# A tuned two-layer hybrid mixer on Trainium2: row-tiled shift products, a 512-wide running maximum and transposed broadcast columns in the attention loop

## The chip, the cores and the metric

One core of one Trainium2 chip runs the whole program. The metric is the device time in microseconds (us). The kernel before took 1449.69 us (median of 3 runs, 1438.94 to 1453.29).

## The reference, cut to what matters

Two layers work on 1024 latent tokens and 256 context tokens of width 1024. Each layer normalises its tokens, multiplies by one combined input projection and sends the slices to four mixers: latent attention, pooling, a state space and a spatial gate. Their outputs are gated and go through one output projection. The change touches the attention alone. Its inputs pass an RMS norm, and it is a softmax attention with 4 heads over 1280 keys for the latent queries (in the first layer also over 256 keys for the context queries):

```python
def _rms(x, g):
    return x * lax.rsqrt(jnp.mean(x * x, -1, keepdims=True) + LN_EPS) * g

s = einsum('bqhd,bkhd->bhqk', qn, k_nope) + einsum('bqhr,bkr->bhqk', qr, k_rope)
p = softmax(s * scale, axis=-1)
o = einsum('bhqk,bkhd->bqhd', p, vf)
```

## The kernel before, in words

Each layer runs in three stages: the input projection with the other mixers' work filled in between (`layer`), the attention loop (`attention`), and the output projection (`out_proj`). Products of float32 values are made of three float32r products (`mm3`: high by high, high by low, low by high).

**The norm (`rms`, L1074).** The squares are summed over features by products with a column of ones (L1084), `r` holds the factor of 128 tokens in each of up to four columns, and L1095 spreads it: a matmul with the column, broadcast to 128 columns, as stationary operand and the identity as moving operand gives a tile in which every row holds the 128 factors. There are 11 such calls (3 for the keys and 3 for the queries in layer 0, 3 and 2 in layer 1) with 38 column spreads in all. They stand in the input-projection stage, where the order of the instructions is a planner's.

**The attention loop (`attention`, L1476 to L1526).** Its order is written out by hand for PE, DVE, ACT and POOL (`manual_schedule`): each engine works in the order of the program. Work is cut into units of 256 queries by one pair of heads (`pairs`). Layer 0 has 8 latent units and 2 context units, layer 1 has 8 latent units. An iteration `w` does one head of a unit, so there are 20 and 16 iterations, of which 32 are full (latent) and 4 short (context). What an iteration does, in the order of the code:

- `scores(v, h, range(1, 5))` (L1314): four banks of scores of the present head, each 128 keys by 2 by 256 queries in one 512-wide PSUM bank, 6 products a bank (L1330). Bank 0 of this head was scored in the iteration before. The running maximum `acc` starts as ACT's copy of bank 0 (`first`, L1338), then DVE takes the maximum with each half of each bank (L1335 to L1340, 8 operations of 256 columns), and folds the two halves (L1342).
- The finish of the unit before and the query projections of the next unit (`finish`, `q_chunk`, `q_pair`) are generators which `go(...)` advances at marked places.
- `vals`: the product of probabilities and values for the head before (`values`, L1400, L1411). It has 5 key-tile pairs, that is 10 products an iteration, two instructions each. `PVS` says how they are cut into three places: 2, 3 and 0 key tiles (3, 2 and 0 in every fourth iteration).
- `maxima` (L1349), after the first place: two PE transposes turn `acc` (L1354), DVE reduces to a maximum for each query (`mx`, L1356), and two small operations make the negated maximum in a high and a low part (`m`, L1358, L1359).
- `rows` (L1361), after the second place: one PE transpose of the four columns (L1365), then one DVE operation makes the rows (`row`, L1367).
- `scores(..., range(0, 1))` for the next head's bank 0 (L1501), then the third place and the `finish` steps: `tp_sm` (L1431, sums over keys) and DVE's reciprocal (L1435).
- `shift` (L1369): five products with a contraction of 4 rows, one on each bank, add the negated maximum to the scores (L1376). Then ACT takes the five exponentials (L1389) into `pE`, `pL`, `pM`, with `first` for the next head after the second of them, and POOL adds them up (`psum`).

The loop draws its PSUM from 5 banks of tag `mm` and 2 of tag `tp`; every sixth score bank is a `tp` bank.

Of the kernel before, what the change touches and what calls it, by code (L numbers as in the profile page):

```python
# [12 lines left out]
F32 = mybir.dt.float32  # L13
F32R = mybir.dt.float32r
I32 = mybir.dt.int32
AF = mybir.ActivationFunctionType
ALU = mybir.AluOpType
AX = mybir.AxisListType
# [15 lines left out]
NPOS = 161  # L34
SEG = 32
PFIX = (1, 2, 3)
PVS = (((0, 2), (2, 5), (5, 5)), ((0, 2), (2, 5), (5, 5)), ((0, 2), (2, 5), (5, 5)), ((0, 3), (3, 5), (5, 5)))
VW = ((0, 1, None), (2, 3, None))
CX = 2
POW = ((0, 4), (4,))  # L40
# [35 lines left out]
def tile_hybrid_backbone(ctx: ExitStack, tc: tile.TileContext, A):  # L76
    nc = tc.nc
    V, S, P, T, D = nc.vector, nc.scalar, nc.gpsimd, nc.tensor, nc.sync

    const = ctx.enter_context(tc.tile_pool(name="const", bufs=1))  # L80
    big = ctx.enter_context(tc.tile_pool(name="big", bufs=1))
    wk = ctx.enter_context(tc.tile_pool(name="wk", bufs=2))
    sml = ctx.enter_context(tc.tile_pool(name="sml", bufs=4))
# [16 lines left out]
    stg = [""]  # L100
# [29 lines left out]
    def tt(e, out, a, b, op):  # L130
        return e.tensor_tensor(out=out, in0=a, in1=b, op=op)  # L131

    def mul(e, out, a, b):
        return tt(e, out, a, b, ALU.mult)

    def add(e, out, a, b):
        return tt(e, out, a, b, ALU.add)
# [4 lines left out]
    def ts(e, out, a, s1, op0, s2_=None, op1=None):  # L142
        if op1 is None:
            return e.tensor_scalar(out=out, in0=a, scalar1=s1, scalar2=None, op0=op0)  # L144
        return e.tensor_scalar(out=out, in0=a, scalar1=s1, scalar2=s2_, op0=op0, op1=op1)  # L145

    def stt(out, a, s, b, op0, op1):
        return V.scalar_tensor_tensor(out=out, in0=a, scalar=s, in1=b, op0=op0, op1=op1)  # L148
# [8 lines left out]
    ident = const.tile([128, 128], F32, name="ident")  # L157
# [4 lines left out]
    V.memset(ones, 1.0)  # L162
    edge = const.tile([128, 2, 18], F32, name="edge")
    D.dma_start(edge, A["edge"])
    rmask = const.tile([4, 2], F32, name="rmask")
    add(V, rmask, ident[0:4, 0:2], ident[0:4, 2:4])
    ones4 = const.tile([4, 128], F32R, name="ones4")
    V.tensor_copy(ones4, ones[0:4, :].to_broadcast([4, 128]))


    cv = s2("cv")[0:16, 0:128]
# [902 lines left out]
    def rms(raws, nfeat, gains):  # L1074

        def go(t0, n):
            nt = n // 128
            stg[0] = "rms"
            ps = tp_ps()
            for j, (x, k) in enumerate(raws):  # L1080
                sq = s2("sq")
                S.activation(out=sq[0:k, 0:n], in_=x[0:k, t0:t0 + n], func=AF.Square)
                for i in range(nt):
                    T.matmul(ps[:, 8 * i + j:8 * i + j + 1], lhsT=sq[0:k, 128 * i:128 * i + 128], rhs=ones[0:k, 0:1],  # L1084
                             start=True, stop=True)
            r = sml.tile([128, 4], F32, tag="rrs", name="rrs")
            pv = ps[:, 0:8 * nt].rearrange("p (i j) -> p i j", j=8)
            ts(V, r[:, 0:nt], pv[:, :, 0], 1.0 / nfeat, ALU.mult, EPS, ALU.add)
            if len(raws) == 2:
                stt(r[:, 0:nt], pv[:, :, 1], 1.0 / nfeat, r[:, 0:nt], ALU.mult, ALU.add)  # L1090
            with tc.high_priority():
                tt(P, r[:, 0:nt], r[:, 0:nt], mhalf.to_broadcast([128, nt]), ALU.pow)
            ps = tp_ps()
            for i in range(nt):
                T.matmul(ps[:, 128 * i:128 * i + 128], lhsT=r[:, i:i + 1].to_broadcast([128, 128]), rhs=ident,  # L1095
                         start=True, stop=True)
            r = ps
            for (x, k), g in zip(raws, gains):
                stt(x[0:k, t0:t0 + n], x[0:k, t0:t0 + n], g, r[0:k, 0:n], ALU.mult, ALU.mult)
        return go  # L1100
# [113 lines left out]
    def attention(l, last, blocks, out):  # L1214
# [99 lines left out]
        def scores(v, h, banks):  # L1314

            c0, pr = pairs[v]
            stg[0] = "sc"
            K, Q = KT[2 * pr + h][(slice(0, 96), slice(0, 128))[h]], prep[v][h]
            if 0 in banks:
                st[v, h] = dict(b=[], acc=s2("acc"))  # L1320
            d = st[v, h]
            acc = d["acc"]
            for i, kts in list(enumerate(BANKS if c0 < NLAT else BANKS[0:1]))[banks.start:banks.stop]:
                ps = tp_ps() if nb[0] % 6 == 5 else mm_ps()
                nb[0] += 1
                d["b"].append(ps)
                for x, kt_ in enumerate(kts):
                    out = ps[:, n * x:n * x + n]
                    for y, (e, f) in enumerate(((0, 0), (0, 1), (1, 0))):
                        T.matmul(out, lhsT=K[:, e, 128 * kt_:128 * kt_ + 128], rhs=Q[:, f], start=(x == 0 and y == 0),  # L1330
                                 stop=False, skip_group_check=True)
                if c0 == NLAT:
                    V.tensor_reduce(out=acc[:, 0:n], in_=ps.rearrange("p (x q) -> p q x", x=2), axis=AX.X, op=ALU.max)
                    continue
                for x in range(2):  # L1335
                    a, p = acc[:, n * x:n * x + n], ps[:, n * x:n * x + n]
                    if i == 0:
                        d["first"] = lambda: S.copy(acc, d["b"][0])  # L1338
                    else:
                        tt(V, a, a, p, ALU.max)  # L1340
                if i == 4:
                    tt(V, acc[:, 0:n], acc[:, 0:n], acc[:, n:2 * n], ALU.max)  # L1342

# [5 lines left out]
        def maxima(v, h):  # L1349
            d = st[v, h]  # L1350
            stg[0] = "mx"
            d["tp"] = tp = tp_ps()
            for j in range(2):
                T.transpose(tp[:, 128 * j:128 * j + 128], d["acc"][:, 128 * j:128 * j + 128], ident)  # L1354
            m = sml.tile([128, 2], F32, tag="mx", name="mx")
            V.tensor_reduce(out=m, in_=tp[:, 0:n].rearrange("p (j k) -> p j k", j=2), axis=AX.X, op=ALU.max)  # L1356
            d["m4"] = m4 = sml.tile([128, 4], F32, tag="m4", name="m4")
            ts(V, m4[:, 0:2].bitcast(F32R), m, -1.0, ALU.mult)  # L1358
            stt(m4[:, 2:4], m, -1.0, m4[:, 0:2], ALU.mult, ALU.subtract)  # L1359

        def rows(v, h):  # L1361

            d = st[v, h]
            tp = d["tp"][0:4, 256:384]
            T.transpose(tp, d["m4"], ident)  # L1365
            d["row"] = row = sml.tile([4, 2, 128], F32R, tag="row", name="row", bufs=2)
            mul(V, row, tp.unsqueeze(1).to_broadcast([4, 2, 128]), rmask.unsqueeze(2).to_broadcast([4, 2, 128]))  # L1367

        def shift(v, h):  # L1369

            c0, pr = pairs[v]
            d = st[v, h]
            stg[0] = "sh"
            rv = d["row"].rearrange("p j q -> p (j q)").unsqueeze(1).to_broadcast([4, 2, n])
            for ps in d["b"]:
                T.matmul(ps, lhsT=ones4, rhs=rv, start=False, stop=True, skip_group_check=True)  # L1376
            e, l1, l2 = wh("pE", F32), None, None
            pt = d["pt"] = [e[:, 0:512], e[:, 512:1024]]
            if c0 < NLAT:
                l1 = wr("pL")  # L1380
                if v < nv - 1:
                    l2 = qp[0].tile([128, 512], F32, tag="pM", name="pM", bufs=3)
                else:
                    if h == 0:
                        st["pM"] = wr("pM")
                    l2 = st["pM"][:, 512 * h:512 * h + 512]
                pt += [l1[:, 0:512], l1[:, 512:1024], l2]
            for i, (ps, p) in enumerate(zip(d["b"], pt)):
                S.activation(out=p, in_=ps, func=AF.Exp, scale=QSCALE)  # L1389
                if i == (1 if c0 < NLAT else 0):  # L1390
                    first(v + h, 1 - h)
            sm = d["sm"] = qp[0].tile([128, 512], F32, tag="psum", name="psum", bufs=3) if v < nv - 1 else s2("psum")
            if c0 < NLAT:
                for i in range(1, 5):
                    add(P, sm, pt[0] if i == 1 else sm, pt[i])
                add(P, sm[:, 0:n], sm[:, 0:n], sm[:, n:2 * n])
            else:
                add(P, sm[:, 0:n], pt[0][:, 0:n], pt[0][:, n:2 * n])
# [77 lines left out]
        with tc.manual_schedule(engines={mybir.EngineType[x] for x in MAN}):  # L1476
            for w in range(2 * nv):
# [13 lines left out]
                    start(q_pair(v + 1, *pairs[v + 1]))  # L1491
                go("mm")
                go("act mm")
                k = [range(5 * h + i, 5 * h + j) for i, j in PVS[w % 4]]
                vals(v, w, k, 0)
                maxima(v, h)
                go("m4")
                vals(v, w, k, 1)
                rows(v, h)
                go("row")  # L1500
                if w + 1 < 2 * nv:  # L1501
                    scores((w + 1) // 2, 1 - h, range(0, 1))
                vals(v, w, k, 2)
                if h and short:
                    go("fend")
# [9 lines left out]
                if w == 2 * nv - 1:  # L1515
                    drop("attq", "att")
                    out.alloc()
                    out.split()
                shift(v, h)
                if w == 2 * fresh[-1] - 3:  # L1520
                    out.scales()
                if w == 2 * nv - 4:
# [528 lines left out]
```

## Time and profile before

| what | value |
|---|---|
| time, median of 3 runs | 1449.69 us (1438.94 to 1453.29) |
| the profiled execution's own time | 1443.26 us |
| its span, first to last instruction | 1441.5 us |
| mean granted TensorE clock, of full speed | 0.940 |
| attention loop of layer 0, in the span | 481 to 672 us |
| attention loop of layer 1, in the span | 1177 to 1339 us |

The span is 1.8 us less than the profiled execution's time. PE is the matmul engine and PEld its weight loads, which overlap with it. In the chain of waits each line is a piece of the path that ended last, with its start, its length and who was at work.

### The profile page before, as it was taken

To read this page: it belongs to the slowest core of one execution; us is meant where nothing else is said; L and a number is where in the kernel's file an instruction comes from. 1 tells how busy PE (TensorE), PEld (TensorE's weight loads), DVE (VectorE), ACT (ScalarE), POOL (GpSimd) and SP (SyncE) were. 2 spreads that over 40 slices of the span, in tenths; PEclk is the share of its full clock that TensorE was granted. 3 is DMA by queue.
4 is the path that set the end of the run, shared out by engine and by line. 5 is a ranking of instruction groups with operands and counts; after the bars stand their busy time and mean duration, and the time that the engine had idled before them with its cause. 6 is when DMAs were issued, how large, how long until landed. Compare 5 with 4: busy or idle time off the path is not lost.

```text
span 1441.5 us, 20269 instructions
## 1 busy us (share of the span) xinstructions
PE 1271.1 (88%) x7558; PEld 992.0 (69%) x7558; DVE 937.8 (65%) x1974; ACT 464.8 (32%) x879; POOL 552.8 (38%) x580
## 2 busy tenths in 40 slices
PE   4877986999999998999999769987699999999997
PEld 1555764779888766766777657765488787766785
DVE  8685399623552576757799882699426447767566
ACT  2341220120343644445233422301213454544300
POOL 2476241301002345655444591314001126656343
PEclk9988997999998999999999979998799999999999
DMA  9435321665321100014122454412752020000421
GB/s 314 143 103 179 122 86 46 152 178 132 89 53 33 27 22 1 1 45 131 45 82 95 107 155 147 122 44 59 149 146 65 8 59 23 15 16 16 146 103 73
DMA packets 124679, 127.33 MB, mean 88 GB/s; under 512 B 40908, under 2 KB 98724, under 8 KB 124582
## 3 DMA queue, kind: packets, MB, share of 16 engines
q1 hardware_dynamic: 118886, 111.86, 26.3%
q0 software_dynamic: 2880, 9.54, 2.8%
q10 hardware_dynamic: 2816, 4.65, 0.9%
q8 instruction: 59, 0.97, 0.3%
q14 instruction: 38, 0.31, 0.1%
HBM read 97.47 MB, written 25.94 MB: 86 GB/s over the span
## 4 chain that ended last, share of the span: by engine, by line
PE 51%; DVE 28%; issue 7%; POOL 6%; DMA 3%; ACT 3%; SPq 1%; POOLq 0%; ACTq 0%; DVEq 0%
PE mm_sc L1330 7%; PE mm_out L1632 6%; PE mm_in L154 5%; PE mm_in L152 5%; DVE H L131 5%; PE mm_in L153 5%; PE av L1411 3%; DVE stmp L131 3%; DVE z L148 3%; PE mm_sc L1376 2%; DVE op L131 2%; DVE acc L131 2%; POOL op L131 1%; DVE xres L145 1%; PE tp_sc L1330 1%
## 5 line engine op out<-in xcount | busy, mean ns | idle before, releaser
L154 PE MATMUL mm_in<-hT,wlo 128*128 128x512 f32 (+1 forms) x696 | 264.6, 381 | 26.9 <-DVE wlo L131 26.9
L152 PE MATMUL mm_in<-hT,whi 128*128 128x512 f32 (+1 forms) x696 | 270.4, 390 | 0.4 <-ACT whi L635 0.4
L153 PE MATMUL mm_in<-hT,whi 128*128 128x512 f32 (+1 forms) x696 | 264.8, 381 | 5.8 <-POOL hT L131 3.1
L154 PEld LDWEIGHTS mm_in<-hT,wlo 128*128 128x128 f32 x696 | 137.6, 198 | 53.3 <-DVE wlo L131 29.4
L152 PEld LDWEIGHTS mm_in<-hT,whi 128*128 128x128 f32 x696 | 137.8, 199 | 35.8 <-issue 14.2
L1632 PE MATMUL mm_out<-wo,yh 128*128 128x512 f32 x576 | 161.4, 394 | 0.5 <-POOL wo L131 0.4
L153 PEld LDWEIGHTS mm_in<-hT,whi 128*128 128x128 f32 x696 | 138.2, 199 | 31.1 <-POOL hT L131 5.7
L1632 PEld LDWEIGHTS mm_out<-wo,yh 128*128 128x128 f32 x576 | 107.5, 189 | 25.5 <-issue 1.0
L635 ACT CAST whi<-wraw 128x1024 fp32r<-128x1024 f32 x38 | 42.6, 1122 | 192.4 <-PE mm_in L153 142.8
L131 DVE TENSOR_TENSOR acc<-acc,mm_sc 128x256 f32<-128x256 f32 x216 | 77.4, 417 | 39.9 <-PE mm_sc L1330 36.8
L131 DVE TENSOR_TENSOR wlo<-wraw,whi 128x1024 fp32r<-128x1024 f32 x38 | 58.0, 1532 | 67.1 <-ACT whi L635 61.0
L131 POOL TENSOR_TENSOR psum<-pE 128x512 f32<-128x512 f32 (+1 forms) x36 | 47.1, 1308 | 135.8 <-ACT pE L1389 135.8
L1632 PE MATMUL mm_out<-wo,yl 128*128 128x512 f32 x288 | 92.0, 392 | 0.6 <-POOL yl L131 0.6
L131 POOL TENSOR_TENSOR psum<-psum,pL 128x512 f32<-128x512 f32 x64 | 83.1, 1298 | 5.0
L131 DVE TENSOR_TENSOR H<-H,stmp 128x80 f32<-128x80 f32 x248 | 75.2, 362 | 0.8
L131 DVE TENSOR_TENSOR stmp<-a,H 128x160 f32<-128x160 f32 x124 | 54.8, 476 | 14.5 <-POOL pws L131 7.2
L144 POOL TENSOR_SCALAR srs<-smv 128x1 f32<-128x1 f32 x18 | 5.6, 312 | 152.6 <-DVE smv L1062 152.6
L1389 ACT ACTIVATE pE<-mm_sc 128x512 f32<-128x512 f32 x55 | 30.6, 594 | 102.3 <-PE mm_sc L1376 102.3
L1632 PEld LDWEIGHTS mm_out<-wo,yl 128*128 128x128 f32 x288 | 54.3, 189 | 12.5 <-POOL yl L131 1.0
L144 POOL TENSOR_SCALAR rs_z<-mv_z 128x1 f32<-128x1 f32 x18 | 18.5, 1029 | 114.7 <-DVE mv_z L1664 114.7
L1783 ACT ACTIVATE G<-mm_in 128x512 f32<-128x512 f32 (+1 forms) x40 | 22.2, 554 | 115.9 <-PE mm_in L154 115.9
L1330 PE MATMUL mm_sc<-QA,KT 96*128 96x256 f32 x372 | 56.8, 305 | 0.0
(360 smaller groups left out, 2805.8 us busy)
## 6 DMA issues: line engine op xcount, KB each, us to landing
wmod<-in_w_mod_dram SPq DMA_DIRECT2D x48, 512.0 KB, 4.5
wraw<-in_w_in_dram SPq DMA_DIRECT2D x36, 512.0 KB, 4.4
wor<-in_w_out_dram SPq DMA_DIRECT2D x16, 512.0 KB, 3.6
s5u<-Sd SPq DMA_DIRECT2D x8, 640.0 KB, 7.1
xd<-z SPq DMA_DIRECT2D x10, 512.0 KB, 2.7
xin<-in_x_dram SPq DMA_DIRECT2D x8, 512.0 KB, 7.6
Ed<-E ACTq DMA_DIRECT2D x16, 256.0 KB, 3.2
Rd<-bldR POOLq DMA_DIRECT2D x16, 256.0 KB, 3.9
```

Source lines behind the costliest of these rows:

```text
L131: return e.tensor_tensor(out=out, in0=a, in1=b, op=op)
L144: return e.tensor_scalar(out=out, in0=a, scalar1=s1, scalar2=None, op0=op0)
L148: return V.scalar_tensor_tensor(out=out, in0=a, scalar=s, in1=b, op0=op0, op1=op1)
L152: T.matmul(out, lhsT=ahi, rhs=bhi, start=start, stop=False)
L153: T.matmul(out, lhsT=ahi, rhs=blo, start=False, stop=False)
L154: T.matmul(out, lhsT=alo, rhs=bhi, start=False, stop=stop)
L635: copy(hi, raw)
L1330: T.matmul(out, lhsT=K[:, e, 128 * kt_:128 * kt_ + 128], rhs=Q[:, f], start=(x == 0 and y == 0), stop=False, skip_group_check=True)
L1376: T.matmul(ps, lhsT=ones4, rhs=rv, start=False, stop=True, skip_group_check=True)
L1389: S.activation(out=p, in_=ps, func=AF.Exp, scale=QSCALE)
L1411: T.matmul(st[v][64 * h:64 * h + 64, 0:n], lhsT=Vt[:, BANKS[i // 2][i % 2], 64 * head:64 * head + 64], rhs=st[v, h]["pt"][i // 2][:, n * ( ...
L1632: T.matmul(a[1][nh], lhsT=y[u][:, k, :], rhs=self.W[k][:, v, 512 * nh:512 * nh + 512], start=(k == 0 and u == 0 and v == 0), stop=(k == KC ...
```

## The change

The diff, cut to its core; tables and lines that stay are left out.

```diff
-PVS = (((0, 2), (2, 5), (5, 5)), ((0, 2), (2, 5), (5, 5)), ((0, 2), (2, 5), (5, 5)), ((0, 3), (3, 5), (5, 5)))
+PVS = ((0, 2), (2, 3), (3, 5))
...
-    rmask = const.tile([4, 2], F32, name="rmask")
-    add(V, rmask, ident[0:4, 0:2], ident[0:4, 2:4])
-    ones4 = const.tile([4, 128], F32R, name="ones4")
-    V.tensor_copy(ones4, ones[0:4, :].to_broadcast([4, 128]))
+    par = const.tile([128, 2], F32, name="par")
+    V.tensor_reduce(out=par[:, 1:2], in_=ident.rearrange("p (c r) -> p r c", r=2)[:, 1:2, :], axis=AX.X, op=ALU.add)
+    ts(V, par[:, 0:1], par[:, 1:2], 2.0, ALU.mult, -1.0, ALU.add)
+    ts(V, par[:, 1:2], par[:, 1:2], -1.0, ALU.mult)
+    ones4 = const.tile([128, 128], F32R, name="ones4")
+    V.tensor_copy(ones4, ones.to_broadcast([128, 128]))
...
-                T.matmul(ps[:, 128 * i:128 * i + 128], lhsT=r[:, i:i + 1].to_broadcast([128, 128]), rhs=ident,
-                         start=True, stop=True)
+                T.transpose(ps[:, 128 * i:128 * i + 128], r[:, i:i + 1].to_broadcast([128, 128]), ident)
...
-                for x in range(2):
-                    a, p = acc[:, n * x:n * x + n], ps[:, n * x:n * x + n]
-                    if i == 0:
-                        d["first"] = lambda: S.copy(acc, d["b"][0])
-                    else:
-                        tt(V, a, a, p, ALU.max)
+                if i == 0:
+                    d["first"] = lambda: S.copy(acc, d["b"][0])
+                else:
+                    tt(V, acc, acc, ps, ALU.max)
...
-            m = sml.tile([128, 2], F32, tag="mx", name="mx")
+            d["m"] = m = sml.tile([128, 2], F32, tag="mx", name="mx")
...
-            d["m4"] = m4 = sml.tile([128, 4], F32, tag="m4", name="m4")
-            ts(V, m4[:, 0:2].bitcast(F32R), m, -1.0, ALU.mult)
-            stt(m4[:, 2:4], m, -1.0, m4[:, 0:2], ALU.mult, ALU.subtract)
...
-            tp = d["tp"][0:4, 256:384]
-            T.transpose(tp, d["m4"], ident)
-            d["row"] = row = sml.tile([4, 2, 128], F32R, tag="row", name="row", bufs=2)
-            mul(V, row, tp.unsqueeze(1).to_broadcast([4, 2, 128]), rmask.unsqueeze(2).to_broadcast([4, 2, 128]))
+            tp = d["tp"][:, 256:512]
+            for j in range(2):
+                T.transpose(tp[:, 128 * j:128 * j + 128], d["m"][:, j:j + 1].to_broadcast([128, 128]), ident)
+            d["row"] = row = sml.tile([128, n], F32R, tag="row", name="row", bufs=2)
+            ts(V, row, tp, par[:, 0:1], ALU.mult)
+            stt(row, tp, par[:, 1:2], row, ALU.mult, ALU.add)
...
-            for ps in d["b"]:
-                T.matmul(ps, lhsT=ones4, rhs=rv, start=False, stop=True, skip_group_check=True)
+            for i, ps in enumerate(d["b"]):
+                r = slice(32 * (i % 4), 32 * (i % 4) + 2)
+                T.matmul(ps, lhsT=ones4[r], rhs=d["row"][r].unsqueeze(1).to_broadcast([2, 2, n]), start=False, stop=True,
+                         skip_group_check=True)
...
-                if w + 1 < 2 * nv:
-                    scores((w + 1) // 2, 1 - h, range(0, 1))
                 vals(v, w, k, 2)
...
                 shift(v, h)
+                if w + 1 < 2 * nv:
+                    scores((w + 1) // 2, 1 - h, range(0, 1))
+                exps(v, h)
```

The maximum of each query is now spread over all 128 partitions by two transposes. Two DVE operations of 256 columns make from it, on every even partition, the negated high part, and on every odd one the negated low part. Each shift product takes two neighbouring partitions, at partition 0, 32, 64 and 96 in turn (the fifth at 0 again), so four of the five lie in four different row groups of the array. `exps` is the rest of the old `shift`: the exponentials and POOL's sums.

## Rows read from the trace of the kernel before

**Rows 1.** The page's first part: busy time and share of each engine.
```profile
PE 1271.1 (88%) x7558; PEld 992.0 (69%) x7558; DVE 937.8 (65%) x1974; ACT 464.8 (32%) x879; POOL 552.8 (38%) x580
```
**Rows 2.** Windows of the two attention loops: length, engines' busy time, clock, DMA.
```profile
481.00:672.00 191.00, 176.16 (x1146) 127.59 (x1144) 128.66 (x286) 90.59 (x181) 107.80 (x95) 0.95 0.08 26
1177.00:1339.00 162.00, 152.19 (x1026) 112.18 (x1027) 111.75 (x256) 79.22 (x155) 97.45 (x84) 0.97 0.07 22
```
**Rows 3.** Chain of waits, a PE-bound iteration of layer 1: start, length, what.
```profile
1230.92 1.01 PE av L1411 x8
1231.94 0.37 PE tp_mx L1354 x2
1232.31 1.45 PE av L1411 x12
1233.76 0.20 PE tp_mx L1365
1233.96 0.70 PE mm_sc L1330 x6
1234.66 1.14 PE mm_sc L1376 x4
1235.80 0.23 PE tp_sc L1376
```
**Rows 4.** Chain of waits, the iteration after it, DVE on the path.
```profile
1241.28 0.44 DVE mx L1356
...
1241.74 0.18 DVE m L144
...
1241.94 0.65 DVE m L148
1242.60 0.33 DVE QA L131
...
1242.96 0.42 DVE QB L131
...
1243.41 0.42 DVE row L131
...
1243.97 0.65 PE tp_sm L1431 x4
1244.62 1.36 PE mm_sc L1376 x5
```
**Rows 5.** Chain of waits: column-divided and undivided products.
```profile
405.04 0.56 PE mm_mod L248 x8
...
1277.42 1.13 PE tp_gl L1577 x4
```
**Rows 6.** Chain of waits, a query projection: a 128-row product, a 64-row one.
```profile
1229.52 0.12 PE tp_q L1226
1229.64 0.31 PE tp_q L1227
```
**Rows 7.** Instructions of L1376: durations in ns, min/median/max.
```profile
L1376 PEld LDWEIGHTS mm_sc<-row,ones x137: 181/183/333, 489.2 to 1335.1; 4*128 4x128 f32 x137
```
**Rows 8.** Groups by form on DVE: busy us, mean ns, idle before.
```profile
L131 DVE TENSOR_TENSOR acc<-acc,mm_sc 128x256 f32<-128x256 f32 x216 | 77.4, 417 | 39.9 <-PE mm_sc L1330 36.8 <-ACT gl L1579 3.0
...
L131 DVE TENSOR_TENSOR z<-mm_out,gl 128x512 f32<-128x512 f32 x30 | 20.4, 681 | 33.9 <-PE mm_out L1632 33.8
...
L145 DVE TENSOR_SCALAR vnt<-mm_sgv,smv,srs 128x256 f32<-128x256 f32 x18 | 9.8, 543 | 14.0 <-POOL srs L131 14.0
...
L148 DVE SCALAR_TENSOR_TENSOR tp_sgu<-tp_sgu,cols,sgw 128x256 f32<-128x256 f32 x18 | 8.5, 484 | 2.1 <-PE tp_sgu L1041 1.9
```
**Rows 9.** Chain of waits: a norm factor's spread in layer 1.
```profile
1127.23 1.16 PE tp_rms L1095 x8
```
**Rows 10.** Chain of waits: value products after a wait in a context iteration.
```profile
528.95 1.91 PE av L1411 x8
```
**Rows 11.** Window of that wait's end: length, engines' busy time, clock, DMA.
```profile
529.00:531.40 2.40, 2.40 (x10) 0.94 (x10) 0.29 (x1) 2.30 (x5) 0.72 (x1) 0.50 0.00 0
```

More of the change, by code (lines that the diff above doesn't have):

```diff
@@ L1354, in maxima, with exps @@
                 T.transpose(tp[:, 128 * j:128 * j + 128], d["acc"][:, 128 * j:128 * j + 128], ident)
-            m = sml.tile([128, 2], F32, tag="mx", name="mx")
+            d["m"] = m = sml.tile([128, 2], F32, tag="mx", name="mx")
             V.tensor_reduce(out=m, in_=tp[:, 0:n].rearrange("p (j k) -> p j k", j=2), axis=AX.X, op=ALU.max)
-            d["m4"] = m4 = sml.tile([128, 4], F32, tag="m4", name="m4")
-            ts(V, m4[:, 0:2].bitcast(F32R), m, -1.0, ALU.mult)
-            stt(m4[:, 2:4], m, -1.0, m4[:, 0:2], ALU.mult, ALU.subtract)
         def rows(v, h):
             d = st[v, h]
-            tp = d["tp"][0:4, 256:384]
-            T.transpose(tp, d["m4"], ident)
-            d["row"] = row = sml.tile([4, 2, 128], F32R, tag="row", name="row", bufs=2)
-            mul(V, row, tp.unsqueeze(1).to_broadcast([4, 2, 128]), rmask.unsqueeze(2).to_broadcast([4, 2, 128]))
-        def shift(v, h):
+            tp = d["tp"][:, 256:512]
[4 more added lines that the diff above has]
+            stt(row, tp, par[:, 1:2], row, ALU.mult, ALU.add)
+        def shift(v, h):
+            d = st[v, h]
+            stg[0] = "sh"
+            for i, ps in enumerate(d["b"]):
+                r = slice(32 * (i % 4), 32 * (i % 4) + 2)
+                T.matmul(ps, lhsT=ones4[r], rhs=d["row"][r].unsqueeze(1).to_broadcast([2, 2, n]), start=False, stop=True,
+                         skip_group_check=True)
+        def exps(v, h):
             c0, pr = pairs[v]
             d = st[v, h]
-            stg[0] = "sh"
-            rv = d["row"].rearrange("p j q -> p (j q)").unsqueeze(1).to_broadcast([4, 2, n])
-            for ps in d["b"]:
-                T.matmul(ps, lhsT=ones4, rhs=rv, start=False, stop=True, skip_group_check=True)
             e, l1, l2 = wh("pE", F32), None, None
@@ L1493, in attention @@
                 go("act mm")
-                k = [range(5 * h + i, 5 * h + j) for i, j in PVS[w % 4]]
+                k = [range(5 * h + i, 5 * h + j) for i, j in PVS]
                 vals(v, w, k, 0)
```

## The prediction

> **What bounds the kernel now.** I read the page first: PE is busy for 88% of the span, no other engine above 65% [rows 1]. The windows by stage come second: the two attention loops, where nearly all of the change lies, take 191 and 162 us, and PE works 176 and 152 us of that at a granted clock of 0.95 and 0.97, so almost all at the 2.4 GHz level [rows 2]. Thirty-six iterations share 353 us, so one takes about 10 us. Third, the chain of waits within the loops. The reader is to see two kinds of iteration. In the first, PE alone is on the chain from the transposes of the maximum to the next scores: 1.45 of values, 0.20 for the rows' transpose, 0.70 for the next head's bank 0, then 1.14 + 0.23 = 1.37 for the five shift products: 3.72 us from the end of the maximum's transposes to the next bank [rows 3]. In the second, DVE is on it: the maximum, the two `m` operations, two subtractions of the query projection (QA, QB), the row, and only then sums and shift: from 1241.26 to 1244.62 + 1.36 = 1245.98, 4.72 us [rows 4]. The second pattern stands in 8 of the 32 full iterations; I price the gain of 20 others by the first, and take nothing for the remaining 4 (the first of each layer, which waits for ACT, the last of layer 1 and the one behind a context unit) and for the 4 short ones.
>
> **Shift products.** Before, five with one contraction of 4 rows take 1.37 us: 0.23 each once running, and about 0.2 for the step into them (1.37 - 5 x 0.23). A like step is seen where a product of 64 rows follows one of 128: 0.31 against 0.12 [rows 6]. After, four lie in different row groups and different banks. The trace shows no row groups side by side, but column groups: eight instructions cut into four column groups of 32 took 0.56 us, 0.07 each, where four undivided ones of the same moving width took 1.13, 0.28 each: 4 times as dense [rows 5]. With 0.2 in, four products in 0.3 and the fifth, back in the first group, in 0.23, I take 0.75. The ends: nothing overlaps, 1.37; or the four run fully together and step in for nothing, 2 x 0.23 = 0.46. I take the value near the column rows because they are the nearest divided products.
> The weights of the five products are loaded into the same 4 rows before, 0.18 us each, and still the products follow each other every 0.23 us [rows 3, 7], so a load into a row group in use is hidden. The Trainium skill ("TensorE: Matmul & The Clock Gate", Part 3: Packing small matmuls — row/col tiling) says that a weight load overlaps running products only when the row group differs. No run here shows the fifth product yet. By the rule it would pay its load of 0.18 in the open; the rows speak against that, and it is the last rival below.
>
> **Transposes for the rows.** One transpose of 0.20 goes [rows 3]; two of 128 columns come, like those of the maximum, 0.37 together [rows 3]. They are queued on PE behind one key tile instead of three. Values take 1.01 for eight instructions and 1.45 for twelve [rows 3], so 0.11 each and 0.13 for the step into column halves; the 4 instructions of one key tile cost 0.57, and the 8 behind the transposes 1.01, with a step of their own. PE's own work from the end of the maximum's transposes to the shift is 0.57 + 0.37 + 1.01 = 1.95.
>
> **DVE between maximum and shift.** The two `m` operations go (0.18 + 0.65 here [rows 4]; the second was short, about 0.16, where POOL didn't run). The row operation of 0.42 goes [rows 4]. Two of 128 x 256 that read PSUM come. Neither has run here. For the scaling the nearest rows are 0.417 for a two-tensor operation and 0.543 for a two-step scaling; for the second, 0.484 [rows 8]. I take 0.42 + 0.48; the ends for both are 0.83 and 1.03. The path from the end of the maximum's transposes: maximum 0.46, handover 0.04, transposes 0.37, 0.42 + 0.48, three handovers together about 0.23 (the gaps between pieces in rows 4 are 0.02 to 0.14): 2.0. PE's own work, 1.95, covers it but for 0.05. So the shift waits on DVE, barely; behind it in PE's queue stand the next head's bank 0 and, through the exponentials, ACT and POOL.
>
> **The next head's bank 0** costs its 0.70 [rows 3] on either side. It covered the row operation before; now it fills the time in which the first exponential frees a bank. With shift at 0.75 plus 0.70, the next banks start 1.45 after the shift's begin, no sooner than before (1.37), so ACT's order of exponentials and copy is met as before. If this cover were gone, up to one exponential would stand open in each iteration.
>
> **The sum of an iteration.** First kind: 2.0 + 0.75 + 0.70 = 3.45 against 3.72, 0.27 less; I take 0.24, since three steps of array shape could each cost a few hundredths more. Times 20: 4.8. Second kind: maximum 0.46, QA and QB 0.33 + 0.42, scaling and row 0.90, handovers 0.26: 2.37; sums of the keys 0.65 (they need the row's PSUM tile, as before); shift 0.75; bank 0 0.70: 4.47 against 4.72, 0.25 less, times 8: 2.0. Sum 6.8.
>
> **The 512-wide maximum.** A bank takes two operations of 0.417 before, one of about 0.681 after [rows 8]: DVE saves 0.15 a bank, some 0.6 an iteration. But it is on the path only behind the last bank, and there the whole bank must now be there first: 0.06 + 0.68 against the 0.77 that the two last halves took where DVE lagged. I take 0.05 in 8 iterations: 0.4. Ends: a loss of 0.2 in each of these, 1.6, and a gain of 2.
>
> **The norm.** Eight instructions, that is four spreads of a float32 product, took 1.16 [rows 9]. A transpose of the same size is one instruction, 0.37 for two [rows 3]: 0.74 for four, 0.42 less. There are 8 calls of four columns and 3 of two: 8 x 0.42 + 3 x 0.21 = 4.0. PE is on the chain at most of them; the last queries of layer 1 wait for POOL, so 3.5. Ends: 0, if DVE and POOL around them set the pace, and 5, as the spreads that fell in a stretch of lower clock were longer.
>
> **The start.** Four small DVE operations replace two, each under the 0.417 of a 256-wide one [rows 8]. DVE waits there for the tokens' load, which hides them; uncovered they would cost about 1 us. No DMA is added, removed or moved. In the stages that a planner orders, other instructions can shift by it: plus or minus 4 us, put in the range.
>
> **Total.** 6.8 + 0.4 + 3.5 = 10.7 us: 1443.3 becomes 1432.6 for the profiled execution. That execution lies 6.4 us below the median of the runs shown, so on the median 1449.7 becomes 1439.
>
> **Rivals.**
> 1. *The row groups don't run together.* For: every product of a lone row group here took 0.23 [rows 3], and no row shows row groups side by side. Against: column groups do [rows 5]. The shift then stays at 1.37, and the row's longer way and the bank-0 cover that is gone are unpaid: 0.35 to 0.4 more in 28 iterations, about 10.5, less 3.9 from norm and maximum: 1456, slower than before. It decides from a shift of about 1.13, where 28 x (1.13 - 0.75) eats the 10.7. Chance 0.13.
> 2. *The groups overlap fully and the short way holds*: shift about 0.5, DVE's two operations at 0.83. The first kind ends near 1.95 + 0.5 + 0.70 = 3.15, 0.57 less, times 20: 11.4; the second 0.5 less, times 8: 4; norm and maximum 4.5: 20 us, 1430. For: the density in rows 5 is already that of four at once. Against: the step into another array shape is paid on each side. Chance 0.27.
> 3. *DVE's wait only moves, and PE's waits lower its clock.* `m` took 0.65 because POOL was at work; QA comes next in DVE's queue and could wait in its stead. In the second kind 0.5 is then lost instead of 0.25 won: 8 x 0.75 = 6 less. And where PE had waited in a context unit, eight values instructions took 1.91 instead of 1.01 [rows 3, 10], at a granted clock of 0.50, the 1.2 GHz level [rows 11]. Context units get a longer bare wait here, as they have few values to put behind the transposes. With 1 us for each of four: 10 less in all, 1449. Chance 0.14.
> 4. *The fifth product's weights aren't loaded ahead*: 0.18 [rows 7] in 28 iterations, 5 less, 1444. Chance 0.05.
> The forecast has the remaining 0.41.
>
> **How the numbers follow.** About 1%, 14.5 us, is what a measurement of this kernel can tell from no change: the lines are 1435.2 and 1464.2. Faster: nearly all of rival 2 (0.26) and a fourth of the forecast (0.11), 0.37. Slower: the part of rival 1 in which the planner's order also goes the wrong way, 0.06, and 0.04 of rival 3: 0.10. The rest, 0.53, is within 1%. The range goes from 1421, rival 2 with a good planner's order, to 1461, rival 1 with a poor one.
>
> **What would show it.** Five shift products near 0.75 in the chain, with starts of the first four some 0.1 or less apart; 4 DVE maxima of about 0.68 an iteration; the row's two operations under 1.0 together; PE waiting under 0.2 before the shift; loops of about 188 and 158 us; four norm transposes in about 0.75. It would be wrong if shift products start 0.23 apart, if the chain shows DVE's row or QA ahead of the shift in most iterations, or if the loops' clock falls.

## The result and the profile after

The changed kernel takes 1431.96 us (median of 18 runs, 1425.49 to 1439.22), and the kernel before 1445.94 us in 18 runs on the same chips: a ratio of 0.990, with a 95% interval of 0.988 to 0.992. That is 14 us less, where 10.7 were forecast. The profiled executions stand at 1430.7 and 1443.26 us. In the page of the kernel after, PE is busy for 19 us less than in [rows 1] and still bounds the kernel:

```profile
span 1428.9 us, 19998 instructions
...
PE 1252.1 (88%) x7556; PEld 962.6 (67%) x7556; DVE 932.5 (65%) x1812; ACT 467.6 (33%) x879; POOL 554.7 (39%) x580
```

To see where the time went I cut both spans at the same events: the first norm product of a layer, its first attention score, and the end of its last shift product. Windows of the kernel after, in the columns of [rows 2]; first and third the norm stages (from first norm product to first score), second and fourth the loops:

```profile
418.60:480.10 61.50, 59.86 (x336) 50.22 (x335) 27.55 (x53) 30.70 (x58) 13.19 (x13) 1.00 0.14 31
480.10:663.50 183.40, 165.88 (x1151) 116.78 (x1149) 119.63 (x198) 89.39 (x177) 106.22 (x94) 0.95 0.07 21
1111.50:1166.20 54.70, 52.93 (x254) 42.70 (x253) 26.47 (x48) 28.70 (x53) 12.44 (x12) 0.94 0.15 34
1166.20:1319.90 153.70, 139.59 (x1030) 99.94 (x1029) 105.68 (x172) 76.71 (x149) 92.89 (x80) 1.00 0.06 20
```

The same windows of the kernel before, cut at these events and so a little shorter than [rows 2]:

```profile
413.40:481.10 67.70, 66.24 (x357) 56.55 (x356) 27.55 (x53) 30.56 (x58) 13.43 (x14) 0.92 0.12 28
481.10:668.90 187.80, 173.07 (x1131) 125.80 (x1129) 125.69 (x282) 87.95 (x177) 106.19 (x94) 0.95 0.07 23
1118.00:1177.40 59.40, 56.46 (x272) 46.49 (x271) 26.71 (x49) 28.80 (x53) 12.45 (x13) 0.91 0.14 32
1177.40:1335.50 158.10, 148.29 (x1015) 109.85 (x1013) 110.45 (x254) 76.33 (x152) 93.87 (x81) 0.99 0.06 19
```

The clock column (one but two from the end) is a mean: most of a norm stage runs at 1.00, the 2.4 GHz level, and one stretch at 0.50, the 1.2 GHz level. The kernel before has some 10 us of it in each norm stage:

```profile
440.00:449.00 9.00, 8.88 (x32) 7.01 (x31) 1.72 (x4) 1.83 (x5) 2.26 (x3) 0.50 0.00 1
1151.00:1160.00 9.00, 9.00 (x34) 8.10 (x33) 2.80 (x6) 2.82 (x7) 3.17 (x3) 0.50 0.31 76
```

The changed kernel has none in the first and some 7 us in the second:

```profile
1145.00:1150.00 5.00, 5.00 (x15) 3.93 (x15) 1.59 (x4) 3.82 (x9) 4.52 (x3) 0.50 0.80 187
```

An input product of the kernel before takes 0.43 in such a stretch and 0.23 right behind it:

```profile
451.36 0.43 PE mm_in L152
451.78 0.23 PE mm_in L153
```

The norm stages gain 6.2 and 4.7, 10.9 us; the loops 4.4 each, 8.8 us. Read off in windows of 2 us, the norm stages had 20.4 us at the lower level before and have 6.8 after, the loops 25.2 and 17.1. If each of these us costs half of itself (an estimate from 0.43 against 0.23), 6.8 of the 10.9 and 4.0 of the 8.8 are clock, and 4.1 and 4.8 are less work on the way. The clock is higher not in this profile alone: the mean over the whole program is 0.945 in the median of the 18 runs, and 0.937 in the median of the kernel before, in each of the four sets of runs beside the experiments. The stretch from the last shift of layer 1 to the end gives 3.0 back (109.0 against 106.0), and the start took 5.2 longer (418.6 against 413.4). The start is left out of the account: in the kernels below it lies anywhere from 412.0 to 418.6, and two kernels that differ in the loop alone, the changed one and *half maxima* (418.6 and 412.5), are as far apart. With 1.1 from the stretch between the layers, 10.9 + 8.8 + 1.1 - 3.0 - 5.2 = 12.6, the span's difference.

An iteration of the first kind, from the chain of waits of the kernel after, to be laid beside [rows 3]:

```profile
1221.37 0.37 PE tp_mx L1354 x2
1221.74 0.58 PE av L1415 x4
1222.32 0.38 PE tp_mx L1363 x2
...
1222.73 0.49 DVE row L144
...
1223.25 0.49 DVE row L148
...
1223.79 0.51 PE mm_sc L1374 x4
1224.30 0.21 PE tp_sc L1374
```

From the end of the maximum's transposes at 1221.74 to the end of the shift at 1224.51 it is 2.77; with the 0.70 of [rows 3] for the next head's bank 0, 3.47, where 3.45 was forecast and 3.72 stood before. The shift (0.51 + 0.21) takes 0.72 instead of 1.37. DVE's two row operations are on the chain here, though PE, with the rest of its values, is done only 0.08 before the shift. The iteration after it has more of DVE on the chain, as in [rows 4]:

```profile
1230.89 0.36 DVE QA L131
...
1231.28 0.84 DVE QB L131
...
1232.16 0.49 DVE row L144
...
1232.68 0.49 DVE row L148
...
1233.22 0.73 PE mm_sc L1374 x5
...
1235.66 0.70 DVE acc L131
...
1236.45 0.70 DVE acc L131
```

Two things are new there. QB takes 0.84 where [rows 4] had 0.42, and the next head's 512-wide maxima follow each other from 1235.66 on with 0.79 between two starts, one long operation waiting for the one before. Among the 195 longest pieces of the chain in each loop, QB stands 13 times on DVE (9 before), and DVE's pieces of `acc` add up to 35.1 us (22.4 before). DVE has come nearer to being the bound. In this iteration the sums over keys aren't on the chain; in most iterations of the second kind they are, as before:

```profile
1191.33 0.38 PE tp_mx L1354 x2
...
1194.53 0.65 PE tp_sm L1435 x4
...
1195.61 0.22 PE mm_sc L1374 x3
```

### The profile page after: what moved, and what is told of

It is laid out like the page before. It is cut to its first block, busy times and chain, and to the rows that moved or that the text cites. A ratio compares the mean times of both kernels' runs of the same rounds, so it can differ in the third digit from the quotient of the medians.

```text
span 1428.9 us, 19998 instructions
## 1 busy us (share of the span) xinstructions
PE 1252.1 (88%) x7556; PEld 962.6 (67%) x7556; DVE 932.5 (65%) x1812; ACT 467.6 (33%) x879; POOL 554.7 (39%) x580
## 4 chain that ended last, share of the span: by engine, by line
PE 51%; DVE 29%; POOL 6%; issue 6%; DMA 4%; ACT 3%; SPq 1%; DVEq 0%; POOLq 0%; ACTq 0%
PE mm_out L1637 7%; PE mm_sc L1332 6%; PE mm_in L154 6%; PE mm_in L152 6%; PE mm_in L153 6%; DVE H L131 5%; DVE stmp L131 3%; DVE z L148 3%; DVE acc L131 2%; PE av L1415 2%; DVE op L131 2%; PE mm_sc L1374 1%; POOL op L131 1%; DMA M<-Kd 1%; DVE xres L145 1%
## 5 line engine op out<-in xcount | busy, mean ns | idle before, releaser
L152 PEld LDWEIGHTS mm_in<-hT,whi 128*128 128x128 f32 x696 | 136.6, 197 | 36.9 <-issue 14.2
L153 PEld LDWEIGHTS mm_in<-hT,whi 128*128 128x128 f32 x696 | 136.5, 196 | 31.4 <-POOL hT L131 5.3
L131 DVE TENSOR_TENSOR acc<-acc,mm_sc 128x512 f32<-128x512 f32 x108 | 74.2, 687 | 42.3 <-PE mm_sc L1332 31.2
L131 POOL TENSOR_TENSOR psum<-pE 128x512 f32<-128x512 f32 (+1 forms) x36 | 47.4, 1318 | 124.2 <-ACT pE L1393 124.1
L1621 ACT CAST yh<-G 128x1024 fp32r<-128x1024 f32 x18 | 18.9, 1052 | 115.1 <-PE mm_out L1637 113.8
```

The source lines that it names most:

```text
L152: T.matmul(out, lhsT=ahi, rhs=bhi, start=start, stop=False)
L153: T.matmul(out, lhsT=ahi, rhs=blo, start=False, stop=False)
```

## The experiments

Twelve edits ran, each in 4 to 12 runs against the kernel before on the same chip. Ratios are to the kernel before, the changed kernel's being 0.990 [0.988, 0.992].

### The norm

**Norm alone.** The kernel before with nothing but the transposes in the norm:

```diff
-                    T.matmul(ps[:, ...], lhsT=r[:, i:i + 1].to_broadcast([128, 128]), rhs=ident, start=True, stop=True)
+                    T.transpose(ps[:, ...], r[:, i:i + 1].to_broadcast([128, 128]), ident)
```

> The kernel before with one edit, the norm's factors spread by transposes. Theory of the forecast: 38 column spreads cost half, about 4 us, of which 3.5 is on the path: 3 to 4.5 us less than before. Rival: the two profiles differ by 6.2 us from the first norm to the first scores in layer 0 and by 4.5 us in layer 1, because the planner puts the input products in another order around shorter norms and the clock stays up there: then 9 to 12 us less than before.

1438.54 us, 0.994 [0.992, 0.997]: 8.5 us, 4.8 to 12.3 by the interval. The forecast for this part was 3.5, with an upper end of 5. Its norm stages in the windows:

```profile
414.20:476.20 62.00, 60.70 (x337) 51.43 (x336) 27.54 (x53) 30.79 (x58) 13.26 (x14) 0.97 0.13 31
1115.70:1170.10 54.40, 52.41 (x254) 42.62 (x253) 26.71 (x49) 28.69 (x53) 12.43 (x12) 0.94 0.15 35
```

They are 5.7 and 5.0 shorter than before, and PE's busy time in them falls by 5.5 + 4.1 = 9.6 us. Two things make it up. A spread of four columns takes 0.65 instead of 1.16 [rows 9], 0.127 a column, times 38 columns: 4.8. In the kernel after, for one:

```profile
1120.60 0.65 PE tp_rms L1098 x4
```

And the mean clock is higher, 0.97 and 0.94 instead of 0.92 and 0.91: 0.05 x 66 + 0.03 x 56 = 5.0 of PE's time. The stretches at 1.2 GHz have gone from 20.4 us to 10.2. The forecast had only the first of the two.

A stretch at the lower level differs between kernels with the same code, so one pair of profiles isn't enough. All the kernels of this document, by the norm that they have:

| norm | kernels | both norm stages, us | of it at 1.2 GHz, us |
|---|---|---|---|
| float32 spread | 3 | 127.1 to 130.5 | 20 to 27 |
| transposes | 7 | 116.2 to 118.9 | 7 to 14 |
| transposes twice | 1 | 124.1 | 17 |
| transposes, wide sums | 3 | 115.5 to 115.7 | 0 |

The first two rows don't touch in either column.

**Norm twice.** The same with each transpose issued twice, so that PE has the old number of instructions again.

```diff
+                for _ in range(2):
                     T.transpose(ps[:, ...], r[:, i:i + 1].to_broadcast([128, 128]), ident)
```

> The kernel before with transposes in the norm, each issued twice, so the array's work for the spread is about 1.5 a call of four columns against 1.16 before and 0.65 to 0.74 with single ones. Theory of the column work: the gain of norm_alone, 8 us, goes altogether, and the stages from the first norm to the first scores are as long as before or longer (68 and 59). Rival, clock: the float32 spread and the gaps around it brought the clock down, and with transposes it stays up whatever their number: the stages stay within 2 us of norm_alone's 62 and 54.

1441.99 us, 0.999 [0.997, 1.001]: the gain is gone. (The profiled execution, 1437.67, lies 4 us under the median.) Windows of the norm stages:

```profile
414.20:478.20 64.00, 62.68 (x356) 53.54 (x355) 27.54 (x53) 30.45 (x58) 13.32 (x13) 0.97 0.13 30
1111.70:1171.80 60.10, 57.81 (x272) 47.13 (x271) 26.53 (x49) 28.60 (x53) 12.43 (x12) 0.89 0.14 31
```

The stages are 7.7 longer than with one transpose. In layer 0 the clock is that of *Norm alone* and the stage 2.0 longer, which is the added work. In layer 1, 5.7 longer, the mean clock falls from 0.94 to 0.89. So in this profile the added instructions come with a loss of clock in one stage and not in the other; the theory of the column work holds in layer 1, the rival in layer 0.

**Old norm.** The changed kernel with the float32 spread of before.

> The kernel after with the norm's factors spread by float32 products again. Forecast's theory: 3 to 4.5 us more than the changed kernel. Rival: 9 to 12 us more, if the planner's order around the norms and the clock there change back as well. The sum with norm_alone tells whether the norm and the loop add up.

1445.6 us, 0.999 [0.997, 1.001]. The norm is worth 13.6 us inside the changed kernel, by the medians, again above the forecast, and the rest of the change alone nothing that can be measured, 4 us at most by the interval: its loops are 2.5 and 1.9 us shorter than before, its norm stages 2.3 longer at a clock of 0.90 and 0.91, its end 3.1 longer. The product of the two parts' ratios, 0.994 x 0.999 = 0.993, is above 0.990, but by no more than the intervals allow.

**Wide sums.** The changed kernel with the norm's sums of squares 64 columns wide instead of one.

```diff
-    T.matmul(ps[:, 8 * i + j:8 * i + j + 1], lhsT=sq[...], rhs=ones[0:k, 0:1], ...)
+    T.matmul(ps[:, 128 * i + 64 * j:128 * i + 64 * j + 64], lhsT=sq[...], rhs=ones[0:k, 0:1].to_broadcast([k, 64]), ...)
```

> The kernel after, with the norm's sums of squares, products of one column, made 64 columns wide (the same sum in each). A weight load of 128 columns bounds them at about 0.10 each either way. Theory: stretches of one-column products are what lets the clock fall in the norm stage (mean 0.94 to 0.95 in most runs of the transposes, 0.91 without): the clock there comes out at 0.98 or more, the two stages 1 to 3 us shorter together. Rival: the wait for the factors lowers the clock, and the stages stay or grow by the wider products, 0 to 3 us.

1431.95 us, 0.991 [0.989, 0.994]. The second stage's clock goes from 0.94 to 1.00 and it is 1.0 us shorter; the first is at 1.00 in either. In that the profile of the changed kernel is an exception: five other kernels with this norm (*No row tiling*, *Bank 0 before*, *Half maxima* and the first two of the section on DVE) have 0.95 in the first stage and 64.0 to 64.1 us, and the three with wide sums 61.8 or 61.9. So wide sums do bring the clock up, for 0.5 to 3.4 us of the two stages, less than the interval of the whole, 4 us to either side, can show.

### The loop

**No row tiling.** The changed kernel with all five shift products in the first row group.

```diff
-                r = slice(32 * (i % 4), 32 * (i % 4) + 2)
+                r = slice(0, 2)
```

> The kernel after, with all five shift products at partitions 0 and 1, so in one row group. Forecast's theory: the four products run side by side only because of the row groups, so the shift goes from 0.73 back to about 1.37 in the chain, 0.6 more in some 28 to 34 iterations: 17 to 20 us more than the changed kernel. Rival: the exponentials on ACT or the maxima on DVE pace the loop, and the shift's length is hidden: under 6 us more.

1464.63 us, 1.012 [1.009, 1.015]: 33 us above the changed kernel, more than the 17 to 20 expected. Chain of waits, a shift in it:

```profile
1251.11 1.19 PE mm_sc L1374 x4
1252.29 0.23 PE tp_sc L1374
```

and the windows of its two loops:

```profile
480.60:680.00 199.40, 183.22 (x1150) 130.84 (x1148) 118.36 (x198) 89.58 (x177) 107.96 (x94) 0.92 0.06 19
1186.20:1355.00 168.80, 156.62 (x1030) 114.69 (x1029) 104.48 (x174) 77.28 (x150) 94.72 (x81) 0.96 0.06 18
```

The shift is back at 1.42, 0.69 more; in 36 iterations that is 25 us at most. The loops are 16.0 and 15.1 longer, so at least 6 more are lost, and the clock in them is lower, 0.92 and 0.96 instead of 0.95 and 1.00 (44 us at the lower level instead of 17). One instruction alone would read the other way: its duration is the longer in the kernel that is faster. Instructions of L1374, ns min/median/max, in the changed kernel:

```profile
L1374 PE MATMUL mm_sc<-row,ones x137: 382/491/792, 488.8 to 1319.9; 2*128 2x512 f32 x137
```

and without row tiling:

```profile
L1374 PE MATMUL mm_sc<-row,ones x137: 382/388/666, 489.3 to 1355.0; 2*128 2x512 f32 x137
```

Five times 0.491 is 2.5 us of durations in a piece of 0.73 on the chain; without row tiling it is 1.94 in 1.42. The recorded durations overlap in both, with row groups far more: the products run side by side.

**Bank 0 before.** The changed kernel with the next head's bank 0 scored ahead of the third place of the values and the shift, as before.

```diff
                 go("row")
+                if w + 1 < 2 * nv:
+                    scores((w + 1) // 2, 1 - h, range(0, 1))
                 vals(v, w, k, 2)
...
                 shift(v, h)
-                if w + 1 < 2 * nv:
-                    scores((w + 1) // 2, 1 - h, range(0, 1))
```

> The kernel after, with the next head's bank 0 scored ahead of the third values place and the shift, as before the change. Forecast's theory: its 0.7 is paid on either side; ahead, it covers DVE's row (a wait of 0.05 to 0.4 in most iterations), but behind the shift of 0.73 the next bank then waits for the first exponential, 0.3 to 0.4: within 5 us of the changed kernel. Rival, the order is what the row tiling needs: 0.4 or more lost in 32 iterations, 12 us or more.

1442.19 us, 0.999 [0.997, 1.001], 10 us slower than the changed kernel, between the 5 at most that were expected and the rival's 12. Chain of waits behind a shift:

```profile
1204.02 0.12 PE mm_sc L1374 x2
1204.13 0.59 ACT pE L1393
...
1204.77 0.99 PE mm_sc L1332 x6
```

PE has nothing to do behind the shift until ACT's first exponential frees a bank: 0.59 us stand open. Ahead of score products (L1332) PE is idle for that reason for 11.7 us in 22 places, in the changed kernel in none:

```profile
  ACT pE L1393: 11.7, 22
```

In the changed kernel bank 0 lies there. So the two edits of the loop need each other. With the norm alone at 0.994, row tiling without the new order comes to 0.999, the new order without row tiling to 1.012, and both together to 0.990. The new cut of the values into places (`PVS`) wasn't tried by itself.

**Half maxima.** The changed kernel with the maximum in two halves of 256.

```diff
...
-                    tt(V, acc, acc, ps, ALU.max)
+                for x in range(2):
+                    a, p = acc[:, n * x:n * x + n], ps[:, n * x:n * x + n]
...
+                        tt(V, a, a, p, ALU.max)
```

> The kernel after, with the running maximum in two halves of 256 columns again. Theory: a 512-wide maximum waits for the one before it on the same tile, 0.79 from start to start where halves alternate and take 0.66 to 0.76 a bank; some 11 iterations have four of these in the chain, so 2 to 5 us less than the changed kernel. Rival, the idea of the edit: fewer operations are less work for DVE, so halves cost 1 to 4 us more.

1433.01 us, 0.990 [0.987, 0.993]: no difference that an interval of some 5 us to either side can show; 2 to 5 less were expected. **Both together**, wide sums and half maxima:

> The changed kernel with both edits that alone made no measurable difference: norm sums 64 columns wide and the maximum in two halves of 256. Theory, neither is on the way that sets the time: 1429 to 1435, a ratio within 0.3% of 0.990. Rival, that each gives back about 1 us where the medians could not show it (the second norm stage was 1.0 us shorter with wide sums; the first of the two halves can start before the bank's second half is scored): 1424 to 1428, a ratio of 0.985 to 0.987.

1429.19 us, 0.990 [0.986, 0.993]: none either.

### DVE's place in the loop

**Subtractions after the rows.** QA and QB stand on the chain ahead of the row. The changed kernel with `go("m4")` moved behind `rows`:

```diff
                 maxima(v, h)
-                go("m4")
                 vals(v, w, k, 1)
                 rows(v, h)
+                go("m4")
```

> The kernel after, with the two subtractions of the query projection (QA, QB) issued on DVE behind the row's two operations instead of ahead of them. In the chain of the changed kernel they stand between the maximum and the row in some 13 of the 32 full iterations, 0.32 to 0.39 and 0.42 to 0.84 each. Theory: the shift waits on DVE there, so each such iteration ends 0.7 to 1.1 sooner: 8 to 13 us less than the changed kernel. Rival: they only move behind, the reciprocal and the next maxima come later by as much, and the time stays within 3 us.

1443.76 us, 0.999 [0.996, 1.001], 12 us slower than the changed kernel where 8 to 13 faster were expected. My theory fell. QB leaves the chain but for one piece on DVE, and the maxima take its place: DVE's pieces of `acc` add up to 49.4 us instead of 35.1, and 4.0 of ACT's come to them. One such stretch in the chain:

```profile
1243.53 0.70 DVE acc L131
...
1244.26 1.13 DVE acc L131
...
1245.52 0.41 PE tp_mx L1354 x2
```

The fold (second row) takes 1.13 where it has 0.42 at its fastest and 0.53 in the median. So DVE seems to be behind in these iterations, and another order of its work only to choose what is late. That is argued from an execution 7 us under the median (1436.38), whose loops are only 3.4 us longer than the changed kernel's; over the 12 runs the median of the mean clock is 0.939 instead of 0.945, so part of the 12 us can be clock.

**Subtractions on POOL.** If that is so, work has to leave DVE. POOL is busy for 39% of the span:

```diff
             for r, q in qs:
-                sub(V, q[r, 1], qf[r], q[r, 0])
+                sub(P, q[r, 1], qf[r], q[r, 0])
```

> The changed kernel with the two subtractions of the query projection (QA, QB) given to POOL in the same place of the program; DVE keeps everything else. POOL stands idle for some 70 us of the first loop until ACT's first exponential, so it has room, and the two aren't needed before the next pair's first scores. If the subtractions on DVE are what delays the row in the 13 iterations that have them on the chain (1.2 us each time), the loops get 8 to 15 us shorter: 1417 to 1424, a ratio of 0.980 to 0.985. Rival, that DVE is behind in those iterations anyhow and only the next of its operations is late in their place, as when they were moved behind the row: the ratio stays within 0.3% of the changed kernel's 0.990. Second rival, that PE's order of work leaves no room for a shorter way, or that POOL's use of the shared port stretches DVE's: slower than the changed kernel by 3 us or more.

1422.92 us, 0.984 [0.982, 0.987]. This beats both kernels: 23 us under the kernel before, 9 under the changed one. The profiled execution, 1428.17, lies 5 us over the median. Windows of its loops:

```profile
479.50:658.70 179.20, 165.74 (x1150) 117.77 (x1148) 111.94 (x180) 89.47 (x177) 119.76 (x114) 0.95 0.07 21
1164.50:1316.80 152.30, 141.07 (x1031) 101.50 (x1030) 98.83 (x158) 76.69 (x149) 103.91 (x96) 0.99 0.07 20
```

The loops are 4.2 and 1.4 shorter at the same clock, and DVE works 14.5 less in them (119.63 + 105.68 against 111.94 + 98.83). On DVE a QB had taken 0.84, as the changed kernel's instructions show (ns min/median/max):

```profile
L131 DVE TENSOR_TENSOR QB<-qp,QB x16: 421/840/1387, 486.7 to 1290.0; 64x256 fp32r<-64x256 f32 x16
```

On POOL it takes 0.72:

```profile
L131 POOL TENSOR_TENSOR QB<-qp,QB x16: 720/722/730, 485.8 to 1288.5; 64x256 fp32r<-64x256 f32 x16
```

It isn't free there: QA now stands 4 times among the longest pieces of the chain, on POOL, ahead of the sums over keys, and DVE's pieces of `acc` add up to 40.9 us. But DVE has lost them both.

**The same in the kernel before**, to see how much of it the change had brought about:

> The kernel before, with nothing of the change, and QA and QB given to POOL. If the changed kernel had made QA and QB what the row waits for (rival 3 of the prediction, the wait of DVE moves from the second row operation to them), the kernel before gains little: QA and QB stood on its chain in 8 iterations for 0.75 us, at most 6 us, and its `m` then still waits for POOL: 1440 to 1446, a ratio of 0.996 to 1.000. Rival, that the gain has nothing to do with the change, DVE being what the loops wait for in either kernel: 7 us or more, a ratio of 0.993 or less. Second rival: POOL's work collides with `m` and the row on the port: slower, above 1.002.

1441.95 us, 0.996 [0.994, 0.999]: 5.5 us, near the 6 at most that QA and QB had on its chain. The gain is 9 in the changed kernel; the intervals overlap too much to say that taking QA and QB off DVE is worth more after the change, though QB itself takes 0.84 in the median on DVE there and 0.42 before.

**POOL's subtractions with wide sums:**

> The changed kernel with QA and QB on POOL (1422.9, ratio 0.984 alone) and with norm sums 64 columns wide (0.991 alone, no different from the changed kernel's 0.990). If the two are independent: 0.984 to 0.985, 1422 to 1424. Rival, that wide sums keep the clock up in the norm stages (1.00 instead of 1.00 and 0.94) and that it tells once the loops are shorter: 0.980 to 0.982, 1417 to 1420. Second rival, that the loops' clock gives it back: 0.987 or more.

1426.3 us, 0.986 [0.983, 0.989]: as with POOL's subtractions alone, and no further gain. It is 6 us under wide sums alone (1431.95), and its loops take 332.4 against 337.4 there, as 331.5 stood against 337.1 without wide sums: the gain on POOL comes back in a second kernel, at 6 to 9 us.

## Why the prediction was right or wrong

The direction was right and the size too small: 10.7 us forecast, 14.0 measured (11.6 to 17.4 by the interval). The predicted 1439 lies 7 above the 1432 measured; 3.8 of that is the median of before, which is 1445.9 over 18 runs and was 1449.7 over the three shown, and 3.3 are the movement.

**The step that failed is the norm's term.** "8 x 0.42 + 3 x 0.21 = 4.0", of which 3.5 were counted, with 5 as the upper end. It measured 8.5 alone, 13.6 inside the changed kernel, and 10.9 in the two stages. The instructions themselves were only a little undersized: 0.127 a spread instead of 0.105, 4.8 in all, as four transposes take 0.65 where 0.74 was forecast. What the term held fixed without a reason is the clock of the stage around them. It took the spread's price from a row at full clock [rows 9] and applied it to stages that ran for some 10 us each at the 1.2 GHz level. Twice in the kernel before, the chain shows what that meant:

```profile
439.30 1.47 PE tp_rms L1095 x8
...
448.52 1.96 PE tp_rms L1095 x8
```

Eight such instructions had cost 1.16 in the row I priced. The prediction named the lower clock and put it only into the upper end, for the spreads alone; a window on the stage would have shown the whole stretch, with input products at 0.43 in it. That the stretch would shrink with the edit could not be read from the trace. The kernels with either norm show that it does, for some 6 us of the norm stages by the estimate above (20 to 27 us at the lower level against 7 to 14); why is open. Taken together, and by that estimate, less work on the way came to 4.1 + 4.8 = 8.9 where 10.7 were forecast; the clock gave 10.8 more in these stages and loops, and the start and the end took 8.2 back.

**Shift products:** right. 0.64 to 0.73 in the chain against 0.75. The neighbour they were priced by, products divided into column groups [rows 5], was a good one. Rival 1 (no overlap) and rival 4 (the fifth product waits for its weights) are out. *No row tiling* is rival 1 made to happen, and worse than priced: its loops are 22.3 longer than before (199.4 + 168.8 against 187.8 + 158.1), where rival 1 said 10.5, and their clock is 0.03 lower in each. Rival 2 (full overlap, shift 0.5) is out as a mechanism, though its 1430 is the nearest number: the missing time came from the norm and the clock.

**Transposes for the rows and DVE's way:** 0.37 was forecast for the two transposes, 0.38 came; 0.42 + 0.48 for the row's two operations, 0.49 + 0.49 came, still under 1.0. An iteration of the first kind came out at 3.47 against 3.45. But one of the prediction's own signs of being wrong came true: DVE's row stands on the chain ahead of the shift in 34 of the 36 iterations (11 before). And PE waits more than the 0.2 that was named: it is idle for the row, ahead of the shift (L1374, the first line) and of the sums over keys (L1435, the second), in 20 iterations for 15.9 us (11 and 5.5 before, with 5.6 more for the `m` operations that are gone):

```profile
  DVE row L148: 8.1, 9
...
  DVE row L148: 7.8, 11
```

**The second kind of iteration** gained nothing where the sums are on the chain: from 1191.71 to 1195.83, for one, it is 4.12, with 0.70 for bank 0 4.82, where 4.47 was forecast and 4.72 stood before. QB's extra 0.42 ate the 0.25.

**The next head's bank 0:** costed at 0.70 on either side, with the warning that without this cover an exponential would stand open. *Bank 0 before* bears it out: 0.59 of ACT on the chain and 10 us.

**The 512-wide maximum:** forecast 0.4, measured nothing. Its operations take 0.69 as their neighbour row said, but follow one another every 0.79, where two halves took 2 x 0.417 = 0.83 [rows 8].

**Rival 3** was half right. DVE's wait did move to QB, 0.84 instead of 0.42, though not for the 0.5 an iteration that it named: 4.82 against 4.72 is 0.1. The clock did not fall: the loops had 0.95 and 0.99 before, 0.95 and 1.00 after, and the values behind the context unit's wait take 1.90, as in [rows 10].

**The loops** were forecast at some 7.2 less and came out 8.8 less (183.4 and 153.7 by the events; 188 and 158 were named for windows 3 to 4 longer). That is partly luck. Three kernels with the old loop (before, *Norm alone*, *Norm twice*) have 343.2 to 350.2 us in the two loops, three with the new (changed, *Old norm*, *Wide sums*) 337.1 to 341.5; with half of the us at the lower level taken off, an estimate, they come to 331.4 to 333.7 and 327.9 to 328.9. So at equal clock the loop's edits are worth some 4 us, and *Old norm*, 4 at most, says the same.

**Not forecast:** the 3 us at the end. In the 17.2 us behind the last shift, PE is busy for 14.3 (16.8 in the kernel before), 31 output products run there instead of 36, and the later ones take 0.233 each instead of 0.228. The kernels with the loop's edits have this stretch at 107 to 109 us, those without at 105 to 106. It wasn't tried to get it back.

## What to carry to other kernels

Read the granted clock along the very stage an edit lies in before pricing it from a row of another: a mean of 0.92 was 10 us at 1.2 GHz and the rest at full clock, and when that stretch shrank with the edit, the stages gained twice what the instructions cost. A product with few rows is worth placing in row groups only if the engine behind it can take the next step sooner, so move the cover along with it. When an off-bound engine's operation stands on the chain, ask whether the engine is late or only the order is wrong: reordering QA and QB cost 12 us, giving them to an idle engine gained 6 to 9.

## What the runs showed that I had not expected

Products run side by side show longer durations (0.491 against 0.388) though the set is done in half the time. Putting the five shift products into one row group cost the loops 31 us, at least 6 more than their own time, with a lower granted clock (0.92 and 0.96 against 0.95 and 1.00). And 38 fewer instructions on PE in two stages of 127 us together shortened them by 10.7 us, twice the instructions' own time, because ten us less of them ran at 1.2 GHz.
